# A recurrent loop whose GpSimd subtractions go to VectorE, with another order around them

## The chip, the cores and the metric

One core of a Trainium2 chip runs the kernel. The metric is device time in microseconds. The engines are named as in the profile: PE is the matrix engine (TensorE), DVE is VectorE, ACT is ScalarE, POOL is GpSimd, and SP issues the DMAs.

## The reference, cut to what matters

The model has two layers over 1040 positions (16 meta tokens and 1024 tokens) of width 1024. The first layer is attention and isn't touched here. The second one, in float32, is:

```
def lru_direction(xc, w_a, b_a, w_x, b_x, lam, reverse):
    r = sigmoid(einsum(xc by blocks of 128, w_a) + b_a)
    i = sigmoid(einsum(xc by blocks of 128, w_x) + b_x)
    log_a = -LRU_C * r * softplus(-lam)
    a = exp(log_a)
    b = sqrt(-expm1(2.0 * log_a)) * i * xc
    h[t] = a[t] * h[t-1] + b[t]          # lax.scan over time, reversed for the second direction

def odd_layer(z, w_in, ...):
    u, gate = split_cols(z @ w_in)       # 2048 columns each
    xc = conv_b + centred depthwise convolution of width 4 over u
    y = lru_direction(xc, forward weights) + lru_direction(xc, backward weights, reverse)
    y = y * silu(gate)
    return y @ w_out
```

## The kernel before

The state lies transposed: channels on the 128 partitions, the 1040 positions along a row. Each matmul is done in three passes, so that two fp32r operands give nearly float32: every operand is split into a high part (the value cast to fp32r) and a rest (value minus high part). `wr` is a weight tile as loaded, `wh` and `wl` its high part and rest, `h1h`/`h1l` those of the layer's input, `oxh`/`oxl` those of the convolution's result `oxc`, `oyh`/`oyl` those of a finished row.

The second layer is a loop over e = 0 to 15, one block of 128 channels in each turn (`class Lru`). A turn works on three blocks at once: `cur` is the block e, whose projections are made, `prev` is the block e-1, whose gates are made, and `late` is the block e-2, whose scans are finished. On PE a turn is: `u_mm(0)`, `u_mm(1)`, `prev.gate(0, 0)`, `u_mm(2)`, `prev.gate(1, 0)`, `g_mm(0)`, `prev.gate(0, 1)`, `g_mm(1)`, `prev.gate(1, 1)`. Here u comes in three chunks of about 347 columns (48 matmuls for the first two, 24 for the third), the silu gate in two chunks of 512 (24 each), and each of the four gates takes 9 or 6 matmuls.

The rest of a turn, with its lines in the profile of before:

- `u_out` (L1201, tile `ou`): VectorE evacuates a u chunk times the row's norm. `conv` (L1208 on ScalarE, L1209 to L1211 on VectorE) makes `oxc` after the third.
- `split_xc` (L768 on ScalarE, L769 on VectorE) makes `oxh` and `oxl`.
- `g_in` (L1221, tile `pg`), `silu` (L1224) and `silu_out` (L1228, tile `otg`) make the silu gate of a chunk.
- `gate` (L1254, L1258) is a tanh on ScalarE, `decay` (L1271, L1272) an exp and a tanh, `root` (L1276) the square root, with a load of another function table ahead of it and one behind. `drive` (L1282, tile `tz`), `mul` (L1262) and `scan_in` (L1287, tile `oz`) make the scan's input on VectorE.
- `scan` (L1292 forward, L1294 reverse), `both` (L1299, the sum of the two) and `gated` (L1303, times the silu gate) finish a row. `keep` and `store` send it to DRAM: rows 0 to 7 as high part and rest (L1315 on ScalarE, L1316 on GpSimd), rows 8 to 13 as they are.

The weights of a turn are five loads of 128x512 into three `wr` buffers: two halves of the g weights, the four gate matrices (`wown`), and two halves of the next turn's u weights. `split_w` casts the high part on ScalarE (L113) and takes the rest on GpSimd (L116). Three PSUM banks, taken in turn, hold the u and g chunks.

The order is written out by hand: from e = 1 on, PE, VectorE, ScalarE and GpSimd each run their instructions in the order of the code, and an engine that waits holds up all that stands behind. SP is ordered by a scheduler up to the loop's end, and by the code after it. Behind the loop stand the last two blocks' gates and scans and the output projection (`oo`, 768 matmuls).

Of the kernel before, what the change touches and what calls it, by code (L numbers as in the profile page):

```python
# [7 lines left out]
F32 = mybir.dt.float32  # L8
F32R = mybir.dt.float32r
# [7 lines left out]
P = 128  # L17
# [24 lines left out]
def trunk_kernel(ctx: ExitStack, tc: tile.TileContext, a: dict, out: bass.AP):  # L42
    nc = tc.nc
# [55 lines left out]
    def split_w(src, shape, nm, own=None, eng=nc.gpsimd, own_bufs=1, raw=None):  # L99
        n = 1  # L100
# [10 lines left out]
        with tc.high_priority(sb.get("ahead", 200)):  # L111
# [4 lines left out]
            eng.tensor_sub(lo[:, :n], raw[:, :n], hi[:, :n].bitcast(F32))  # L116
# [1047 lines left out]
    def w_gates(e):  # L1164
        return split_w(a["wg"][e], (4, P), "wg", "gw", own_bufs=2)
# [4 lines left out]
    def w2_half(e, isu, hf):  # L1170
        return split_w(a["w2"][2 * e + isu, hf], (4, P), "w2")

    def w2_load(e, isu):
        return [w2_half(e, isu, hf) for hf in range(2)]
# [11 lines left out]
    class Lru:  # L1186
# [26 lines left out]
        def split_xc(self):  # L1213
            self.c = split(self.xc, "ox", "X")
# [20 lines left out]
        def weights(self):  # L1235
            self.w = w_gates(self.e)
# [73 lines left out]
        def store(self):  # L1310

            e, yv = self.e, self.z[1]
            if e < 8:
                hi, lo = row("oyh", "X", F32R), row("oyl", "X", F32R)
                nc.scalar.copy(hi[:, :1024], yv[:, :1024])  # L1315
                nc.gpsimd.tensor_sub(lo[:, :1024], yv[:, :1024], hi[:, :1024].bitcast(F32))  # L1316
# [45 lines left out]
    for e in range(16):  # L1362
# [5 lines left out]
        if e == 0:  # L1368
# [22 lines left out]
            cur.split_xc()  # L1391
# [5 lines left out]
        else:  # L1397
            w_g = w2_load(e, 0)
            cur.weights()
# [4 lines left out]
            if late:  # L1404
                prev.silu_out(1)
                late.mul(1)
                late.scan_in(1)
            cur.u_mm(1, w_u)
            cur.u_out(1)
            if late:  # L1410
                late.scan(1)
                late.both()
# [7 lines left out]
            if late:  # L1420
                late.gated()
            if e < 15:
                if late:
                    late.keep()
                w_u = [w2_half(e + 1, 1, 0)]
# [3 lines left out]
            if e < 15:  # L1429
                prev.root()  # L1430
                cur.g_in(0, cur.g_mm(0, w_g))
                prev.drive(0)
                prev.drive(1)
                prev.gate(0, 1)
                w_u.append(w2_half(e + 1, 1, 1))
# [4 lines left out]
                cur.split_xc()  # L1440
                if late:
                    late.store()
                cur.g_in(1, cur.g_mm(1, w_g))
                cur.silu(1)
                prev.gate(1, 1)
                late, prev = prev, cur
# [6 lines left out]
    for e in range(4):  # L1453
        y_load(e)
    late.keep()
    cur.split_xc()
# [3 lines left out]
    prev.gate(0, 1)  # L1460
    w_o = [split_w(a["wo2"][d, 0], (4, P), "wo2", raw=raw_o[d]) for d in range(3)]
# [12 lines left out]
    prev.gate(1, 1)  # L1474
# [160 lines left out]
```

## Time and profile before

| | |
|---|---|
| median of 3 runs | 1867.83 us (1867.34 to 1867.99) |
| profiled execution | 1866.78 us, of which the span is 1864.9 us |
| PE busy | 1803.3 us, 97% of the span |
| VectorE busy | 1229.8 us, 66% |
| ScalarE busy | 877.3 us, 47% |
| GpSimd busy | 802.1 us, 43% |
| granted clock of PE | 0.997 |

The span runs from the first instruction to the last; the execution has 1.9 us around it. The recurrent loop with its manual order (e = 1 to 15) takes the stretch from about 1242 to 1675 us, and the output projection follows it. Matmuls overlap, so a busy PE in the table does not say that none of its time is lost. Times in the rows are microseconds from the start of the span.

### The profile page before, as it was taken

How to read it: one execution, taken by the hardware profiler on the slowest of the kernel's cores; microseconds unless marked ns; L12 is line 12 of the kernel's file. 1: busy time of each engine (PE TensorE's matmuls, PEld its weight loads, DVE VectorE, ACT ScalarE, POOL GpSimd, SP SyncE). 2: the span in 40 equal slices, each digit the busy share in tenths (PEclk: the TensorE clock that was granted, in tenths of full speed). 3: DMA queues.
4: the chain of work that ended last, by engine and by line, in shares of the span. 5: the costliest groups of instructions: out<-in, count | busy, mean ns of one | idle time of the engine just before them, and what ended most of it. 6: DMA issues, size and time to landing. Idle time of an engine off the chain costs nothing.

```text
span 1864.9 us, 28561 instructions
## 1 busy us (share of the span) xinstructions
PE 1803.3 (97%) x10822; PEld 1641.8 (88%) x10822; DVE 1229.8 (66%) x1956; ACT 877.3 (47%) x1490; POOL 802.1 (43%) x713
## 2 busy tenths in 40 slices
PE   8999989989999999999999999999999999999999
PEld 7997888889999999888888889998888889988887
DVE  8687357787764641678777774348988989989000
ACT  5455224445443210466667652127776676674000
POOL 5446365354322463357555433332433433326331
PEclk9999999999999999999999999999999999999999
DMA  5355532223222363323222103422222222136421
GB/s 181 81 191 185 164 92 69 62 60 103 61 84 93 137 184 115 117 69 93 70 75 75 41 24 117 145 70 60 76 80 74 95 72 77 60 131 254 143 77 41
DMA packets 109333, 186.47 MB, mean 100 GB/s; under 512 B 31951, under 2 KB 51535, under 8 KB 109198
## 3 DMA queue, kind: packets, MB, share of 16 engines
q1 hardware_dynamic: 109198, 184.67, 31.2%
q8 instruction: 85, 1.39, 0.3%
q14 instruction: 50, 0.41, 0.1%
HBM read 126.72 MB, written 49.92 MB: 95 GB/s over the span
## 4 chain that ended last, share of the span: by engine, by line
PE 69%; DVE 16%; ACT 7%; POOL 5%; issue 2%; DMA 1%; SPq 0%; DVEq 0%; POOLq 0%; ACTq 0%
PE pj L168 12%; PE oo L168 10%; PE pxop L168 6%; PE pg L1183 5%; PE px L935 5%; PE pu L1183 5%; PE av L1026 4%; PE tp L998 3%; PE op L168 3%; PE up L168 3%; PE pz L128 2%; PE vps L435 2%; PE py L935 2%; DVE oxl L769 1%; DVE oz L1287 1%
## 5 line engine op out<-in xcount | busy, mean ns | idle before, releaser
L116 POOL TENSOR_TENSOR wl<-wr,wh 128x512 fp32r<-128x512 f32 (+2 forms) x218 | 320.8, 1475 | 301.9 <-ACT wh L113 269.8
L115 POOL TENSOR_SCALAR wh<-wr 128x512 fp32r<-128x512 f32 (+2 forms) x157 | 121.6, 775 | 376.0 <-PE pj L168 124.4
L168 PE MATMUL pj<-xh,wl 128*128 128x346 f32 (+1 forms) x768 | 251.3, 328 | 14.3 <-DVE wl L116 7.8
L168 PE MATMUL pj<-xl,wh 128*128 128x346 f32 (+1 forms) x768 | 249.1, 324 | 0.9 <-DVE xl L269 0.8
L168 PE MATMUL pj<-xh,wh 128*128 128x346 f32 (+1 forms) x768 | 248.9, 324 | 0.0
L168 PEld LDWEIGHTS pj<-xh,wl 128*128 128x128 f32 x768 | 146.5, 191 | 16.1 <-ACT xh L268 7.7
L168 PEld LDWEIGHTS pj<-xl,wh 128*128 128x128 f32 x768 | 146.6, 191 | 2.0 <-DVE xl L269 1.9
L168 PEld LDWEIGHTS pj<-xh,wh 128*128 128x128 f32 x768 | 146.6, 191 | 0.1
L1183 PE MATMUL pu<-h1h,wl 128*128 128x346 f32 (+1 forms) x384 | 125.2, 326 | 6.3 <-DVE ou L1201 3.3
L1183 PE MATMUL pu<-h1l,wh 128*128 128x346 f32 (+1 forms) x384 | 123.5, 322 | 0.0
L1183 PE MATMUL pu<-h1h,wh 128*128 128x346 f32 (+1 forms) x384 | 123.4, 321 | 0.0
L1013 ACT CAST pth<-tp 128x512 fp32r<-128x512 f32 (+1 forms) x160 | 77.9, 507 | 66.2 <-PE tp L998 52.3
L1014 DVE TENSOR_TENSOR ptl<-tp,pth 128x512 fp32r<-128x512 f32 (+1 forms) x160 | 90.2, 585 | 19.9 <-ACT pth L1013 16.4
L1183 PE MATMUL pg<-h1h,wl 128*128 128x512 f32 x256 | 101.4, 396 | 0.0
L168 PE MATMUL oo<-oyh,wh 128*128 128x512 f32 x256 | 101.1, 395 | 0.0
L1183 PE MATMUL pg<-h1h,wh 128*128 128x512 f32 x256 | 101.1, 395 | 0.0
L1183 PE MATMUL pg<-h1l,wh 128*128 128x512 f32 x256 | 100.8, 394 | 0.0
L168 PE MATMUL oo<-oyh,wl 128*128 128x512 f32 x256 | 100.6, 393 | 0.0
L168 PE MATMUL oo<-oyl,wh 128*128 128x512 f32 x256 | 100.4, 392 | 0.0
L944 ACT ACTIVATE p<-py,mmx,msc 128x256 f32<-128x256 f32 (+1 forms) x72 | 40.8, 567 | 119.0 <-DVE mmx L942 102.3
L1351 DVE TENSOR_TENSOR hres<-oo,hres 128x512 f32<-128x512 f32 x16 | 10.6, 688 | 129.0 <-PE oo L168 129.0
L998 PE MATMUL tp<-ident,p 128*128 128x128 f32 (+1 forms) x576 | 90.5, 275 | 2.7 <-POOL p L955 1.9
(446 smaller groups left out, 5471.2 us busy)
## 6 DMA issues: line engine op xcount, KB each, us to landing
wr<-in_w SPq DMA_DIRECT2D x128, 256.0 KB
wr<-in_wo SPq DMA_DIRECT2D x64, 256.0 KB
s_g<-gth SPq DMA_DIRECT2D x10, 520.0 KB
xr<-in_x SPq DMA_DIRECT2D x8, 520.0 KB
s_qn<-qr SPq DMA_DIRECT2D x8, 520.0 KB
s_kn<-kr SPq DMA_DIRECT2D x8, 520.0 KB
sw<-qraw SPq DMA_DIRECT2D x16, 260.0 KB
yb<-s_yb SPq DMA_DIRECT2D x8, 520.0 KB
```

The source lines that it names most:

```text
L115: eng.tensor_scalar(hi[:, :n], raw[:, :n], 1.0, 1.0, ALU.mult, ALU.mult)
L116: eng.tensor_sub(lo[:, :n], raw[:, :n], hi[:, :n].bitcast(F32))
L128: nc.tensor.matmul(ps[:m, off + c0:off + c1], w, x[:, c0:c1], start=first and j == 0 and pi == 0, stop=last and j == nt - 1 and pi == 2)
L168: nc.tensor.matmul(t[:, :c1 - c0], w, x[:, c0:c1], start=first and j == 0 and pi == 0, stop=last and j == nt - 1 and pi == 2)
L435: nc.tensor.matmul(ps[:m, :n], s, w, start=j == 0 and pi == 0, stop=j == nt - 1 and pi == 2)
L935: nc.tensor.matmul(dst[:m, d0:d0 + a1 - a0], l[:, s], r[:, a0:a1], start=pi == 0, stop=pi == 4)
L944: nc.scalar.activation(p_[:m, b0:b1], ps, AF.Exp, bias=mx[:m, 2:3], scale=sc, accum_out=mx[:m, 3 + z:4 + z])
L998: nc.tensor.transpose(tp[:, o:o + m], p_[:m, NM + P * (kt + j):NM + P * (kt + j) + P], ident[:m, :m])
L1013: nc.scalar.copy(hi[:, :w], tp[:, :w])
L1014: nc.vector.tensor_sub(lo[:, :w], tp[:, :w], hi[:, :w].bitcast(F32))
L1026: nc.tensor.matmul(av[:, :n], l[:, vs], pts[kt][o][:, j * n:j * n + n], start=kt == 0 and j == 0 and pi == 0, stop=False)
L1183: nc.tensor.matmul(t[:, :c1 - c0], l, r[:, c0:c1], start=hf == 0 and k == 0 and pi == 0, stop=hf == 1 and k == 3 and pi == 2)
```

## The change

Four things change in the recurrent loop; the rest of the kernel keeps its instructions and their order.

1. The rests of the five weight tiles of a turn are subtracted on VectorE instead of GpSimd, and so is the rest of a stored row. `split_w` gets a list `later`, into which it puts the subtraction; the loop calls it where it should stand in VectorE's order (`rests[0]` to `rests[4]`). GpSimd keeps one memset of 128x16 a turn.
2. `split_xc` becomes `xc_hi` and `xc_lo`; the last g chunk's `g_in` (the third input chunk of the title) stands between them, and its `silu_out` moves from the next turn to the end of this one.
3. `late.both` moves from behind the reverse scan to behind the third `u_out`, and `late.gated` and `late.keep` to behind the convolution and the fourth rest. The load and cast of the second half of the next u weights move up, from behind `prev.gate(0, 1)` to behind `prev.root`.
4. Behind the loop, `late.gated` stands ahead of the split of the last `oxc`, and `prev.gate(1, 1)` directly behind `prev.gate(0, 1)` instead of behind the last silu.

```
-    def split_w(src, shape, nm, own=None, eng=nc.gpsimd, own_bufs=1, raw=None):
+    def split_w(src, shape, nm, own=None, eng=nc.gpsimd, own_bufs=1, raw=None, later=None):
...
-            eng.tensor_sub(lo[:, :n], raw[:, :n], hi[:, :n].bitcast(F32))
+            rest = lambda e: e.tensor_sub(lo[:, :n], raw[:, :n], hi[:, :n].bitcast(F32))
+            if later is None:
+                rest(eng)
+            else:
+                later.append(lambda: rest(nc.vector))
...
-        def split_xc(self):
-            self.c = split(self.xc, "ox", "X")
+        def xc_hi(self):
+            self.c = row("oxh", "X", F32R), row("oxl", "X", F32R)
+            nc.scalar.copy(self.c[0], self.xc)
+
+        def xc_lo(self):
+            nc.vector.tensor_sub(self.c[1], self.xc, self.c[0].bitcast(F32))
...
-                nc.gpsimd.tensor_sub(lo[:, :1024], yv[:, :1024], hi[:, :1024].bitcast(F32))
+                nc.vector.tensor_sub(lo[:, :1024], yv[:, :1024], hi[:, :1024].bitcast(F32))
...
-            w_g = w2_load(e, 0)
-            cur.weights()
+            rests = []
+            w_g = w2_load(e, 0, rests)
+            cur.weights(rests)
             if late:
                 late.scan(0)
             cur.u_mm(0, w_u)
             cur.u_out(0)
             if late:
-                prev.silu_out(1)
                 late.mul(1)
                 late.scan_in(1)
+            rests[0]()
+            rests[1]()
             cur.u_mm(1, w_u)
             cur.u_out(1)
+            rests[2]()
             if late:
                 late.scan(1)
-                late.both()
...
             cur.u_out(2)
             if late:
-                late.gated()
+                late.both()
             if e < 15:
-                if late:
-                    late.keep()
-                w_u = [w2_half(e + 1, 1, 0)]
+                w_u = [w2_half(e + 1, 1, 0, rests)]
             cur.conv()
             prev.gate(1, 0)
             prev.decay(1)
             if e < 15:
+                rests[3]()
+                if late:
+                    late.gated()
+                    late.keep()
                 prev.root()
+                w_u.append(w2_half(e + 1, 1, 1, rests))
                 cur.g_in(0, cur.g_mm(0, w_g))
                 prev.drive(0)
                 prev.drive(1)
+                rests[4]()
                 prev.gate(0, 1)
-                w_u.append(w2_half(e + 1, 1, 1))
                 cur.silu(0)
                 prev.mul(0)
                 prev.scan_in(0)
                 cur.silu_out(0)
-                cur.split_xc()
+                cur.xc_hi()
+                cur.g_in(1, cur.g_mm(1, w_g))
+                cur.xc_lo()
                 if late:
                     late.store()
-                cur.g_in(1, cur.g_mm(1, w_g))
                 cur.silu(1)
                 prev.gate(1, 1)
+                cur.silu_out(1)
                 late, prev = prev, cur
...
+    late.gated()
     late.keep()
-    cur.split_xc()
+    cur.xc_hi()
+    cur.xc_lo()
...
     prev.gate(0, 1)
+    prev.gate(1, 1)
...
-    prev.gate(1, 1)
     prev.mul(1)
```

What this makes of VectorE's order in the middle of a turn, from the reverse scan (L1294 before, L1302 in the change; both are printed by their operands) to the drives, is seen in two pieces. Before:

```order
L1294 SCALAR_TENSOR_TENSOR oz<-oa,oz 128x1024
L1299 TENSOR_TENSOR oz<-oz 128x1024
L1201 TENSOR_TENSOR ou<-pu,rstd 128x346
L1303 TENSOR_TENSOR oz<-oz,otg 128x1024
L1209 SCALAR_TENSOR_TENSOR oxc<-ou,vec,oxc 128x1038
L1210 SCALAR_TENSOR_TENSOR oxc<-ou,vec,oxc 128x1039
L1211 SCALAR_TENSOR_TENSOR oxc<-ou,vec,oxc 128x1039
L1221 SCALAR_TENSOR_TENSOR pg<-pg,rstd 128x512
L1282 SCALAR_TENSOR_TENSOR tz<-oa,tz 128x1040
L1282 SCALAR_TENSOR_TENSOR tz<-oa,tz 128x1024
```

The same place in the change:

```order
L1302 SCALAR_TENSOR_TENSOR oz<-oa,oz 128x1024
L1205 TENSOR_TENSOR ou<-pu,rstd 128x346
L1307 TENSOR_TENSOR oz<-oz 128x1024
L1213 SCALAR_TENSOR_TENSOR oxc<-ou,vec,oxc 128x1038
L1214 SCALAR_TENSOR_TENSOR oxc<-ou,vec,oxc 128x1039
L1215 SCALAR_TENSOR_TENSOR oxc<-ou,vec,oxc 128x1039
L116 TENSOR_TENSOR wl<-wr,wh 128x512
L1311 TENSOR_TENSOR oz<-oz,otg 128x1024
L1229 SCALAR_TENSOR_TENSOR pg<-pg,rstd 128x512
L1290 SCALAR_TENSOR_TENSOR tz<-oa,tz 128x1040
L1290 SCALAR_TENSOR_TENSOR tz<-oa,tz 128x1024
L116 TENSOR_TENSOR wl<-wr,wh 128x512
```

The third evacuation of u has moved ahead of the sum, the gated product behind the convolution, and two weight rests have come in, one of them behind the drives.

From the end of one turn to the next reverse scan VectorE's order of before is:

```order
L769 TENSOR_TENSOR oxl<-oxc,oxh 128x1040
L1221 SCALAR_TENSOR_TENSOR pg<-pg,rstd 128x512
L1292 SCALAR_TENSOR_TENSOR oz<-oa,oz 128x1040
L1201 TENSOR_TENSOR ou<-pu,rstd 128x348
L1228 SCALAR_TENSOR_TENSOR otg<-otg,pg 128x512
L1262 SCALAR_TENSOR_TENSOR oz<-pz,oxc 128x1024
L1287 TENSOR_TENSOR oz<-oz,tz 128x1024
L1201 TENSOR_TENSOR ou<-pu,rstd 128x346
```

In the change, for a turn that stores a row, the same stretch is:

```order
L1229 SCALAR_TENSOR_TENSOR pg<-pg,rstd 128x512
L1222 TENSOR_TENSOR oxl<-oxc,oxh 128x1040
L1324 TENSOR_TENSOR oyl<-oz,oyh 128x1024
L1236 SCALAR_TENSOR_TENSOR otg<-otg,pg 128x512
L1300 SCALAR_TENSOR_TENSOR oz<-oa,oz 128x1040
L1205 TENSOR_TENSOR ou<-pu,rstd 128x348
L1270 SCALAR_TENSOR_TENSOR oz<-pz,oxc 128x1024
L1295 TENSOR_TENSOR oz<-oz,tz 128x1024
L116 TENSOR_TENSOR wl<-wr,wh 128x512 x2
L1205 TENSOR_TENSOR ou<-pu,rstd 128x346
L116 TENSOR_TENSOR wown<-wr,wown 128x512
```

The last g chunk's evacuation and its silu product have moved ahead of the forward scan, the stored row's rest has come in ahead of it, and three weight rests stand around the second evacuation of u.

On ScalarE, behind the root, the cast of the second half of the next u weights has moved ahead of the table load and the tanh of the next gate. Before:

```order
L1276 ACTIVATE tz<-tz 128x2080
L1258 ACT_TABLE_LOAD
L1258 ACTIVATE pz<-pz,hb 128x1040
L113 CAST wh<-wr 128x512
L1224 ACTIVATE otg<-pg 128x512
```

In the change:

```order
L1284 ACTIVATE tz<-tz 128x2080
L113 CAST wh<-wr 128x512
L1266 ACT_TABLE_LOAD
L1266 ACTIVATE pz<-pz,hb 128x1040
L1232 ACTIVATE otg<-pg 128x512
```

The cast and the tanh have changed places, and the table load stays with the tanh.

## Rows read from the trace of the kernel before

**Rows 1.** Windows: start:end, length, then busy time of each engine.

```profile
1356.80:1386.40 29.60, 28.83 (x151) 25.27 (x151) 26.91 (x22) 20.56 (x22) 11.42 (x7) 1.00 0.24 81
1591.70:1620.10 28.40, 28.40 (x152) 25.35 (x152) 26.25 (x23) 20.52 (x21) 9.33 (x7) 1.00 0.20 65
```

**Rows 2.** Chain of waits: start, length, engine, tile and line.

```profile
1563.59 7.63 PE pu L1183 x48
...
1572.65 3.85 PE pu L1183 x24
...
1648.60 7.63 PE pu L1183 x48
```

**Rows 3.** Timeline of PE, first matmuls of turns e = 1, 4 and 12.

```profile
1242.56 0.32 PE L1183 MATMUL pu<-h1h,wl 128*128 128x348 f32 x1
...
1327.48 0.33 PE L1183 MATMUL pu<-h1h,wl 128*128 128x348 f32 x1
...
1563.43 0.32 PE L1183 MATMUL pu<-h1h,wl 128*128 128x348 f32 x1
```

**Rows 4.** Timeline of PE in turn e = 6: idle time before, and what ended it.

```profile
1388.79 0.43 PE L1183 MATMUL pu<-h1h,wl 128*128 128x348 f32 x1 [0.30 <-POOL wl L116]
...
1396.65 0.43 PE L1183 MATMUL pu<-h1h,wl 128*128 128x346 f32 x1 [0.45 <-DVE ou L1201]
```

**Rows 5.** Timeline of VectorE, turns e = 5 and 6.

```profile
1370.65 2.96 DVE L1294 TENSOR_TENSOR_SCAN oz<-oa,oz 128x1024 f32<-128x1024 f32 x1
1373.64 2.13 DVE L1299 TENSOR_TENSOR oz<-oz 128x1024 f32<-128x1024 f32 x1
1375.70 0.50 DVE L1201 TENSOR_TENSOR ou<-pu,rstd 128x346 f32<-128x346 f32 x1
...
1384.40 2.38 DVE L1282 SCALAR_TENSOR_TENSOR tz<-oa,tz 128x1040 f32<-128x1040 f32 x2 [2.28 <-ACT tz L1276]
1386.82 1.24 DVE L1262 SCALAR_TENSOR_TENSOR oz<-pz,oxc 128x1040 f32<-128x1040 f32 x1
1388.09 1.74 DVE L1287 TENSOR_TENSOR oz<-oz,tz 128x1040 f32<-128x1040 f32 x1
...
1390.36 3.00 DVE L769 TENSOR_TENSOR oxl<-oxc,oxh 128x1040 fp32r<-128x1040 f32 x1
...
1398.36 1.50 DVE L1287 TENSOR_TENSOR oz<-oz,tz 128x1024 f32<-128x1024 f32 x1
...
1405.27 0.50 DVE L1201 TENSOR_TENSOR ou<-pu,rstd 128x346 f32<-128x346 f32 x1
```

**Rows 6.** Timeline of VectorE, turns e = 14 and 15.

```profile
1647.99 1.23 DVE L769 TENSOR_TENSOR oxl<-oxc,oxh 128x1040 fp32r<-128x1040 f32 x1
...
1657.33 2.27 DVE L1294 TENSOR_TENSOR_SCAN oz<-oa,oz 128x1024 f32<-128x1024 f32 x1
1659.63 1.23 DVE L1299 TENSOR_TENSOR oz<-oz 128x1024 f32<-128x1024 f32 x1
```

**Rows 7.** Timeline of GpSimd, turns e = 5 and 6.

```profile
1371.79 2.91 POOL L116 TENSOR_TENSOR wl<-wr,wh 128x512 fp32r<-128x512 f32 x1 [0.28 <-ACT wh L113]
1387.45 1.29 POOL L116 TENSOR_TENSOR wl<-wr,wh 128x512 fp32r<-128x512 f32 x1 [12.75 <-ACT wh L113]
1389.84 2.41 POOL L1316 TENSOR_TENSOR oyl<-oz,oyh 128x1024 fp32r<-128x1024 f32 x1 [1.11 <-ACT oyh L1315]
```

**Rows 8.** Groups of VectorE in the first 60 us: busy time, mean ns.

```profile
L116 DVE TENSOR_TENSOR wl<-wr,wh 128x512 fp32r<-128x512 f32 x2 | 1.4, 688 | 0.0
```

**Rows 9.** Timeline of ScalarE, turn e = 5.

```profile
1371.11 0.60 ACT L113 CAST wh<-wr 128x512 fp32r<-128x512 f32 x1
```

**Rows 10.** Timeline of SP's DMA issues, turn e = 5.

```profile
1367.99 7.06 SPq L96 DMA_DIRECT2D wr<-in_w  x4
```

**Rows 11.** Timeline of VectorE, end of turn e = 15 and behind the loop.

```profile
1668.47 1.24 DVE L769 TENSOR_TENSOR oxl<-oxc,oxh 128x1040 fp32r<-128x1040 f32 x1 [1.13 <-ACT oxh L768]
1671.73 2.38 DVE L1282 SCALAR_TENSOR_TENSOR tz<-oa,tz 128x1040 f32<-128x1040 f32 x2 [2.02 <-ACT tz L1276]
```

More of the change, by code (lines that the diff above doesn't have):

```diff
@@ L1162, in trunk_kernel, with w_gates, w2_half, w2_load @@
     CHR = ((16, 528), (528, 1040))
-    def w_gates(e):
-        return split_w(a["wg"][e], (4, P), "wg", "gw", own_bufs=2)
+    def w_gates(e, later=None):
+        return split_w(a["wg"][e], (4, P), "wg", "gw", own_bufs=2, later=later)
     def halves(t, o=0):
         return [(t[:, 0:512], o, o + 512), (t[:, 512:1024], o + 512, o + 1024)]
[L1170 to L1174, printed above, removed]
+    def w2_half(e, isu, hf, later=None):
+        return split_w(a["w2"][2 * e + isu, hf], (4, P), "w2", later=later)
+    def w2_load(e, isu, later=None):
+        return [w2_half(e, isu, hf, later) for hf in range(2)]
     def chunk_mm(w, halfs, t, c0, c1):
@@ L1233, in g_mm, with weights @@
             return t
-        def weights(self):
-            self.w = w_gates(self.e)
+        def weights(self, later=None):
+            self.w = w_gates(self.e, later)
         def gate(self, d, j):
@@ L1454, in trunk_kernel @@
         y_load(e)
+    late.gated()
     late.keep()
-    cur.split_xc()
+    cur.xc_hi()
+    cur.xc_lo()
     prev.root()
```

## The prediction

> **What bounds the kernel now.** I read the busy times first, then the windows, the chain of waits and the timelines. The matrix engine (PE) is busy in 97% of the span (the table above), so only a stretch where it stands still can give time back. Cut by turn of the recurrent loop, the turn e = 5 takes 29.6 us and PE's modelled busy time is 28.83, while turn e = 13 takes 28.4 with PE busy throughout [rows 1]. The chain of waits shows why: in the late turns it runs through PE alone, and three turns from 1563.59 to 1648.60 take 85.01 us, 28.34 a turn [rows 2]. That is PE's floor, since the change takes no matmul away. The eight turns e = 4 to 11 lie between the PE rows 1327.48 and 1563.43 [rows 3]: 235.95 us against 8 x 28.34 = 226.72. So 9.2 us stand to be won in the whole loop: the three turns before them (1242.56 to 1327.48, 28.31 each) and the last ones are already at the floor.
>
> Where PE stands in such a turn, the PE timeline names [rows 4]. The second half of the next u weights waits for GpSimd's subtraction, and the third u chunk waits for VectorE to evacuate the first chunk (`ou`). That evacuation is late because VectorE's own round is too long. From the third `ou` evacuation (1375.70) to the next one (1405.27) is 29.57 us [rows 5]. Of this, 8.70 us go to ScalarE, which makes the convolution's start, the decays and the root, until `tz` is released at 1384.40; the remaining 20.87 us are one VectorE instruction after another. This round, and not PE, sets the turn.
>
> **GpSimd's part.** The same operations are short where GpSimd is idle [rows 6]: the rest of xc (`oxl`) 1.23 us, the reverse scan 2.27, the sum 1.23. In the long turn they take 3.00, 2.96 and 2.13 [rows 5], each while a GpSimd subtraction of two SBUF tiles runs [rows 7]: `wl` from 1371.79 for 2.91 us lies over scan and sum, `oyl` from 1389.84 for 2.41 over `oxl`. Operations that read PSUM don't show it. The two products (L1287) take 1.74 and 1.50, where I take 1.23, the price of the same shapes undisturbed.
>
> The Trainium skill (SBUF — State Buffer, "Who interferes with whom") says that a VectorE operation with two SBUF inputs and a GpSimd operation that reads SBUF exclude each other, and that whichever starts first keeps the port while the other waits. The trace agrees that they collide, but not on who pays: the scan began at 1370.65, before GpSimd's 1371.79, and still took 2.96. Strictly by that rule the scan's 0.69 excess would not be GpSimd's and would stay: the round worked out below would be 28.57, which leaves 8 x 0.23 = 1.8 us of the loss, a time of 1860.4. The row with GpSimd idle decides, and I take 2.27.
>
> **The new VectorE round, step by step.** Taken off the 20.87: `oxl` 1.77, scan 0.69, the two products 0.51 and 0.27 (1.50 to 1.23). The sum also leaves this stretch: it now stands behind the third `ou`, beside ScalarE's 8.70, so its whole 2.06 goes (1373.64 to 1375.70). Together 5.30.
>
> Added to it: subtractions of 128x512. VectorE's own row for exactly this is 0.688 us [rows 8]; the next instruction begins about 0.07 before the last one ends (1373.64 + 2.13 is 0.07 past 1375.70), so one costs 0.62. The far bound is GpSimd's undisturbed price, 1.29 [rows 7]; I take the near one, since it is the same engine, shape and types. Three stand at the head of the turn: 1.86. The fourth stands behind the convolution beside ScalarE's work. The fifth stands behind the two drives: 2.31 + 0.62 = 2.93 after 1384.40. There the product with xc would wait anyway, because the cast of the second half now lies between root and table load on ScalarE: that wait was 2.42 (1386.82 less 1384.40) and gets about 0.6 longer [rows 5, 9]. So the fifth and that cast together cost 0.6. In turns e = 2 to 9, where a finished row is stored, the rest `oyl` adds 1.23 - 0.08 = 1.15. Sum 3.61.
>
> The round becomes 8.70 + 20.87 - 5.30 + 3.61 = 27.9 us in storing turns, 26.7 in the others. Both lie below 28.34: PE becomes the bound everywhere, with 0.45 us to spare where it is tightest. With the far bound, 1.29 a subtraction, the four would add about 2.5: rounds of 30.4 and 29.2, and a time of about 1879, slower than before. VectorE's own row excludes that as far as a row can.
>
> **What hides the rest.** The first drive stands 8.70 behind the third `ou`. In that time VectorE now has: sum, then from ScalarE's first result (1.8) three convolution steps of 1.3, the fourth subtraction, the gated product (1.2) and the gate's chunk 0.6: 8.2. If that cover went, the excess over 8.70 would be added to the round one for one. Evacuating the third pg chunk ahead of `oxl` moves an instruction of 0.6 within the round and costs nothing. The `silu_out` of that chunk moves ahead of the forward scan. PE's third u chunk, which takes its PSUM bank, starts 9.06 into a turn and lasts 3.85 [rows 2], so the third `ou` stands at 13.1 of a turn; the `silu_out` ends some 18.3 later, at 3.1 of the next turn, 6 us before the bank is wanted. The second stall of rows 4 thus goes. For the first: the last weight rest is now done 8.70 + 2.93 = 11.6 after the third `ou`, at 24.7, and PE wants it in the next turn, after 28.34.
>
> Queues: the loads (`wr`, three buffers) are now released by VectorE. SP issues in order; the tightest one is the next u half, released by the turn's first subtraction at about 8.7 (13.1 + 27.9 less the scan, two subtractions and an evacuation that follow it, 4.0, less 28.34). Its cast on ScalarE stands ahead of the convolution's start and cannot begin before PE has finished the third u chunk, at 13.0. That leaves 4.3 us. Today the load is issued at 1367.99 [rows 10] and cast at 1371.11 [rows 9] without a wait for DMA: at most 3.1. The other four have more.
>
> The end: the last turn's gate moves six matmuls ahead of the second g halves, on the same engine; the gated product (1.2, or 2.3 if GpSimd collides) lies ahead of `oxl`, which idled 1.13 for ScalarE, and the drive behind it idled 2.0 more [rows 11]. I count nothing.
>
> **Sum.** The profiled execution took 1866.78; less 9.2 is 1857.6. The median of the runs is 1.05 higher: 1858.6.
>
> **Rivals.**
> - *VectorE's round stays the longest in storing turns.* For it: only 0.45 us are spare over some 25 instructions. At 0.04 more for each the round is 28.9 and eight turns keep 8 x 0.55 = 4.4 us: 1863.0. Against: nearly every price is a row of this kernel.
> - *A new wait eats the gain.* The change would do its work on VectorE, but PE then waits for a cast or a bank that I counted as early: 1 us a turn in eight turns leaves 1867, the same.
> - *Slower: the load behind the released buffer.* If it lands later than 4.3 + 0.45 us after its issue, each further us delays cast, convolution and round in all turns e = 2 to 14. From 5.5 us on the gain is gone (13 x 0.7 = 9.1), at 6.5 us the time is about 1881. Against: 3.1 is a ceiling, and no wait for a load is seen in these turns.
> - *VectorE stands still after each added instruction.* With its length paid twice (four of 0.69, one of 1.23) the round is 31.9, in the other turns 29.5: 8 x 3.5 + 5 x 1.1 - 9.2 = 24 us slower, 1892. Rows 5 speak against it: the next instruction begins before the last has ended. The Trainium skill (VectorE: DVE Perf Modes, "The DRAIN you can't avoid") says that an idle flush of about the duration less 266 ns follows each operation; no row here shows such a pause.
>
> **How the numbers follow.** Forecast 0.72 (its own range 1857.6 to 1860.4, which takes in the scan's 1.8), longer round 0.14, eaten gain 0.08, late load 0.05, pause 0.01. The range 1857.3 to 1863.2 takes the forecast and most of the longer round. A change of 0.2%, 3.7 us, is about what a measurement can tell here. Faster: 0.72 plus 0.12 of the longer round; same: 0.02 of it plus 0.08; slower 0.06.
>
> **What would show it.** Right: turns of 28.3 us throughout, PE without a stop between the first u chunk and the output projection, `oxl`, sum and scan at 1.23, 1.23 and 2.3, GpSimd with nothing but the 128x16 memsets, VectorE waiting again for PE ahead of the third `ou`. Wrong: `wl` on VectorE above 0.8 us, or ScalarE waiting for a load ahead of a weight cast, or any turn above 28.6.

## The result, and the profile after

| | before | after |
|---|---|---|
| median | 1867.59 us (4 runs) | 1858.22 us (4 runs, 1856.47 to 1859.21) |
| profiled execution | 1866.78 us | 1858.87 us |
| span | 1864.9 us | 1857.1 us |
| granted clock of PE | 0.997 | 0.996 |

The change is faster: the ratio is 0.9949, with a 95% interval of 0.9936 to 0.9963. The medians lie 9.4 us apart, and 1858.6 us had been forecast.

Where the time comes from is read from PE's first matmul of the turns e = 1, 4 and 12, as in [rows 3]. PE's timeline after, with start, length, engine and instruction:

```profile
1242.93 0.32 PE L1187 MATMUL pu<-h1h,wl 128*128 128x348 f32 x1
...
1327.85 0.33 PE L1187 MATMUL pu<-h1h,wl 128*128 128x348 f32 x1
...
1554.26 0.32 PE L1187 MATMUL pu<-h1h,wl 128*128 128x348 f32 x1
```

The eight turns e = 4 to 11 now take 1554.26 - 1327.85 = 226.41 us, 28.30 each, where they took 235.95: 9.54 us. From the turn e = 1 to the turn e = 15 no turn is longer than 28.34 or shorter than 28.27. The windows of the turns e = 5 and 13, the columns as in [rows 1]:

```profile
1356.10:1384.40 28.30, 28.30 (x151) 25.29 (x150) 27.00 (x28) 20.60 (x21) 0.11 (x1) 1.00 0.27 87
1582.70:1611.00 28.30, 28.30 (x151) 25.32 (x151) 25.69 (x28) 19.64 (x20) 0.11 (x1) 1.00 0.21 66
```

PE is busy throughout in both. VectorE's busy time hardly moved in the turn e = 5 (26.91 before, 27.00 after) although six instructions were added to it (x22 to x28), and GpSimd's fell from 11.42 us to 0.11, one memset. VectorE's timeline of the turns e = 5 and 6 answers to [rows 5]; the figure in brackets is the idle time ahead of an instruction and what ended it:

```profile
1366.52 2.28 DVE L1302 TENSOR_TENSOR_SCAN oz<-oa,oz 128x1024 f32<-128x1024 f32 x1
1369.21 0.52 DVE L1205 TENSOR_TENSOR ou<-pu,rstd 128x346 f32<-128x346 f32 x1 [0.41 <-PE pu L1187]
1369.65 1.22 DVE L1307 TENSOR_TENSOR oz<-oz 128x1024 f32<-128x1024 f32 x1
...
1377.93 2.38 DVE L1290 SCALAR_TENSOR_TENSOR tz<-oa,tz 128x1040 f32<-128x1040 f32 x2 [0.56 <-ACT tz L1284]
1380.23 0.68 DVE L116 TENSOR_TENSOR wl<-wr,wh 128x512 fp32r<-128x512 f32 x1
1380.86 1.24 DVE L1270 SCALAR_TENSOR_TENSOR oz<-pz,oxc 128x1040 f32<-128x1040 f32 x1
1382.13 1.24 DVE L1295 TENSOR_TENSOR oz<-oz,tz 128x1040 f32<-128x1040 f32 x1
...
1384.49 1.23 DVE L1222 TENSOR_TENSOR oxl<-oxc,oxh 128x1040 fp32r<-128x1040 f32 x1
1385.64 1.22 DVE L1324 TENSOR_TENSOR oyl<-oz,oyh 128x1024 fp32r<-128x1024 f32 x1
...
1397.52 0.52 DVE L1205 TENSOR_TENSOR ou<-pu,rstd 128x346 f32<-128x346 f32 x1 [0.60 <-PE pu L1187]
```

VectorE now waits for PE ahead of the third `ou` (0.41 and 0.60 us), so the round from one third `ou` to the next, 28.31, is PE's. How long it would be by itself shows in the first two storing turns, where VectorE runs late and waits for nothing there. The same timeline, turns e = 2 to 4:

```profile
1286.00 0.48 DVE L1205 TENSOR_TENSOR ou<-pu,rstd 128x346 f32<-128x346 f32 x1
...
1313.53 0.49 DVE L1205 TENSOR_TENSOR ou<-pu,rstd 128x346 f32<-128x346 f32 x1
...
1341.12 0.49 DVE L1205 TENSOR_TENSOR ou<-pu,rstd 128x346 f32<-128x346 f32 x1
```

The rounds are 27.53 and 27.59 us, 27.56 on the mean, against 29.57 before. The prices, which answer to [rows 6, 8], stand in VectorE's groups by shape, turns e = 2 to 14 (busy time, mean ns of one, idle time before):

```profile
L116 DVE TENSOR_TENSOR wl<-wr,wh 128x512 fp32r<-128x512 f32 x53 | 35.2, 684 | 0.0
L1302 DVE TENSOR_TENSOR_SCAN oz<-oa,oz 128x1024 f32<-128x1024 f32 x13 | 29.7, 2282 | 0.0
L1222 DVE TENSOR_TENSOR oxl<-oxc,oxh 128x1040 fp32r<-128x1040 f32 x14 | 17.2, 1230 | 0.0
L1307 DVE TENSOR_TENSOR oz<-oz 128x1024 f32<-128x1024 f32 x13 | 15.8, 1214 | 0.0
```

The table of waits from 1240 to 1690 us (engine and tile, what it waited for: us in total, times, longest) has no row in which a u or g matmul of PE waits, where [rows 4] stood. ScalarE waited once for a load, in the turn e = 2:

```profile
DVE ou L1205 <- PE pu L1187: 12.1, 11, 1.7
...
ACT wh L113 <- DMA wr<-in_w: 0.7, 1, 0.7
```

Not all of the loop's gain reaches the span, which is 7.8 us shorter. From the first u matmul of e = 1 to that of e = 15 it is 9.68 (405.88 to 396.20). The loop starts 0.37 later in this execution, the stretch from the last turn to the output projection is the same (34.25), and the projection takes 179.25 us instead of 177.87. A new wait stands in it, in PE's timeline:

```profile
1692.19 0.40 PE L172 MATMUL oo<-oyh,wl 128*128 128x512 f32 x1
1693.08 0.50 PE L172 MATMUL oo<-oyl,wh 128*128 128x512 f32 x1 [0.49 <-DMA oyl<-s_yl]
```

These matmuls start every 0.23 us; here the step is 0.89, so 0.66 is lost to the load of a stored row's rest. The other 0.7 of the 1.4 us belongs to no single wait.

### The profile page after: what moved, and what is told of

Read it like the earlier page. It is cut to its first block, busy times and chain, and to the rows that moved or that the text cites. A ratio compares the mean times of both kernels' runs of the same rounds, so it can differ in the third digit from the quotient of the medians.

```text
span 1857.1 us, 28484 instructions
## 1 busy us (share of the span) xinstructions
PE 1801.4 (97%) x10822; PEld 1642.6 (88%) x10822; DVE 1232.5 (66%) x2037; ACT 877.6 (47%) x1490; POOL 660.0 (36%) x632
## 4 chain that ended last, share of the span: by engine, by line
PE 80%; DVE 8%; POOL 5%; ACT 3%; DMA 2%; issue 2%; SPq 0%; DVEq 0%; POOLq 0%; ACTq 0%
PE pj L172 13%; PE pu L1187 10%; PE pg L1187 10%; PE oo L172 9%; PE pxop L172 7%; PE px L939 5%; PE pz L132 5%; PE av L1030 4%; PE tp L1002 3%; PE op L172 3%; PE up L172 3%; PE vps L439 2%; PE py L939 2%; PE av L757 1%; PE sps L697 1%
## 5 line engine op out<-in xcount | busy, mean ns | idle before, releaser
L116 POOL TENSOR_TENSOR wl<-wr,wh 128x512 fp32r<-128x512 f32 (+2 forms) x160 | 229.5, 1436 | 61.6 <-PE pg L1187 49.4
L172 PEld LDWEIGHTS pj<-xh,wl 128*128 128x128 f32 x768 | 147.0, 192 | 14.8 <-ACT xh L272 6.9
```

Source lines behind the costliest of these rows:

```text
L116: rest = lambda e: e.tensor_sub(lo[:, :n], raw[:, :n], hi[:, :n].bitcast(F32))
L172: nc.tensor.matmul(t[:, :c1 - c0], w, x[:, c0:c1], start=first and j == 0 and pi == 0, stop=last and j == nt - 1 and pi == 2)
```

## The experiments

Each kernel was timed beside the kernel before on the same chip, and the ratios to it are what is compared; the median of before shown is that beside the change. "Eight turns" runs from the first u matmul of e = 4 to that of e = 12, "round" from one third `ou` on VectorE to the next in a storing turn in which VectorE doesn't wait for PE there.

| kernel | median, us | ratio (95% interval) | eight turns, us | round, us |
|---|---|---|---|---|
| before | 1867.59 | | 235.95 | 29.57 |
| after | 1858.22 | 0.9949 (0.9936 to 0.9963) | 226.41 | 27.56 |
| `order_only` | 1857.47 | 0.9944 (0.9929 to 0.9959) | 226.41 | 27.52 |
| `vector_only` | 1864.75 | 0.9986 (0.9977 to 0.9995) | 231.23 | 28.97 |
| `sum_only` | 1858.01 | 0.9954 (0.9939 to 0.9968) | 226.41 | 27.39 |
| `sum_line` | 1860.34 | 0.9960 (0.9945 to 0.9974) | 226.41 | 27.40 |
| `sum_back` | 1864.24 | 0.9979 (0.9969 to 0.9989) | 229.79 | 28.88 |
| `waits_only` | 1889.76 | 1.0123 (1.0108 to 1.0138) | 249.24 | 30.97 |
| `one_more` | 1858.06 | 0.9949 (0.9933 to 0.9966) | 226.41 | 28.33 |
| `three_more` | 1875.29 | 1.0046 (1.0029 to 1.0063) | 237.87 | 29.78 |
| `gate_back` | 1860.04 | 0.9957 (0.9942 to 0.9972) | 226.41 | 27.56 |

`row_on_pool` (one execution, 1860.20 us) and `pool_beside_scan` (one, 1858.05 us) have 226.40 and 226.41 us in the eight turns.

### Which half of the change: `order_only` and `vector_only`

`order_only` is the changed kernel with every subtraction back on GpSimd:

```
-                later.append(lambda: rest(nc.vector))
+                rest(eng)
+                later.append(lambda: None)
...
-                nc.vector.tensor_sub(lo[:, :1024], yv[:, :1024], hi[:, :1024].bitcast(F32))
+                nc.gpsimd.tensor_sub(lo[:, :1024], yv[:, :1024], hi[:, :1024].bitcast(F32))
```

> The changed order, but all subtractions (five weight rests, the stored row's rest) left on GpSimd. My theory (a VectorE round that only has to fall below PE's 28.34 us): of the 29.57 the sum's 2.06 goes beside ScalarE, the cast ahead of the table load adds 0.6, so 28.1, up to 28.7 if the sum and the gated product collide with GpSimd: turns of 28.3 to 28.7, time 1858 to 1861. The rival (GpSimd's collisions are what cost the time): oxl at 3.0 and the scan at 2.96 remain, turns of 29 us or more, time 1864 to 1867.

`vector_only` is the kernel before with the subtractions on VectorE, at about the places where they stand in the change (the fifth stands behind the product and the `scan_in` of the forward direction, since its cast comes later in the old order), and everything else in its old place:

```
+                later.append(lambda: rest(nc.vector))
...
-                nc.gpsimd.tensor_sub(lo[:, :1024], yv[:, :1024], hi[:, :1024].bitcast(F32))
+                nc.vector.tensor_sub(lo[:, :1024], yv[:, :1024], hi[:, :1024].bitcast(F32))
...
+            rests[0]()
+            rests[1]()
             cur.u_mm(1, w_u)
             cur.u_out(1)
+            rests[2]()
...
             prev.decay(1)
             if e < 15:
+                rests[3]()
                 prev.root()
...
-                w_u.append(w2_half(e + 1, 1, 1))
+                w_u.append(w2_half(e + 1, 1, 1, rests))
...
                 prev.scan_in(0)
+                rests[4]()
```

> The old order, with the subtractions on VectorE at about the places that the change gives them. My theory: 4.1 us of collisions go (oxl 1.77, sum 0.90, scan 0.69, products 0.78), 3.6 us of subtractions come, round 29.1 instead of 29.57: turns of about 29.1 in e = 4 to 11, time about 1864, so most of the gain is missing. The rival: GpSimd's relief alone is the gain, turns of 28.3, time 1858 to 1859.

The order alone gives the whole gain, with GpSimd as busy as before: all turns are 28.3, and the rival of `order_only` (turns of 29 or more) falls. The engine alone gives half of it in the eight turns (4.7 of 9.5 us) and less of the time: the ratio of 0.9986 is 2.6 us (0.9 to 4.3 by its interval), and the rival of `vector_only` (all of the gain) falls. Its round is 28.97, above PE's 28.3, and PE waits for a weight rest again, as the waits of `vector_only` show:

```profile
PE pu L1187 <- DVE wl L116: 3.3, 8, 0.5
```

So taking GpSimd out is not needed for the gain, and alone it doesn't reach it. What in the order does it had to be found.

### What in the order: `sum_only`, `sum_line`, `waits_only`, `sum_back`

`sum_only` is the kernel before with the sum behind the third `ou`, and the gated product and `keep` (which sends the rows 8 to 13 to DRAM; the expectation calls it the gate's chunk) behind the convolution:

```
                 late.scan(1)
-                late.both()
...
             cur.u_out(2)
             if late:
-                late.gated()
+                late.both()
             if e < 15:
-                if late:
-                    late.keep()
                 w_u = [w2_half(e + 1, 1, 0)]
...
             prev.decay(1)
             if e < 15:
+                if late:
+                    late.gated()
+                    late.keep()
                 prev.root()
...
+    late.gated()
     late.keep()
```

> The kernel before with one thing of the new order alone: the sum (`both`) moves behind the third `ou`, and the gated product and the gate's chunk (`gated`, `keep`) behind the convolution; the subtractions stay on GpSimd, `silu_out(1)` and the u weights' second half stay where they were. Theory (the length of VectorE's round sets the turn): the sum's 2.06 us leave the stretch behind the drives, the round falls from 29.57 to 27.5, below PE's 28.34, and all turns are 28.3: about 1858 us, the whole gain from a few moved lines, and the two waits seen in the turn e = 6 (PE for `wl`, PE for the first `ou`) go although nothing about `wl` or the bank was moved. Rival (those two places, the weight rest and the bank's release, are the cause): they still wait, turns stay at 29 or more, 1864 to 1868 us.

`waits_only` is the kernel before with two other moves instead, those that are meant to take away the two waits of [rows 4] by name:

```
-                prev.silu_out(1)
                 late.mul(1)
...
                 prev.root()
+                w_u.append(w2_half(e + 1, 1, 1))
...
                 prev.gate(0, 1)
-                w_u.append(w2_half(e + 1, 1, 1))
...
                 prev.gate(1, 1)
+                cur.silu_out(1)
```

> The kernel before with the other half of the new order alone: `silu_out(1)` moves from the head of the next turn to the end of its own, and the load, cast and rest of the u weights' second half move ahead of the drives; sum, gated product and chunk stay where they were. VectorE's round keeps all its instructions. Theory (the round sets the turn): the round stays near 29.57, 1.23 above PE's 28.34, so the third `ou` drifts 1.2 us a turn later in its turn as before; PE's stalls can begin a turn or two later because the bank is released earlier, and behind that the turns are 29.6 again: 1861 to 1866 us. Rival (the two named waits are the cause): with them gone all turns are 28.3 and the time is about 1858 us.

`sum_only` has the whole gain. In `waits_only` the round did not stay as I expected: it grew to 30.97, and the turns follow it (about 31 each in e = 4 to 6, then 32.5 and 29.4 in turn). The loop lost 15.9 us on the kernel before and the tail 6.2, so the time missed the expected 1861 to 1866 by far. PE still waits for the weight rest in some turns, and for the very `silu_out` that was issued earlier:

```profile
PE pu L1183 <- DVE otg L1228: 16.0, 12, 1.9
...
PE pu L1183 <- POOL wl L116: 1.0, 5, 0.2
```

VectorE's timeline in it shows where most of the 1.4 us come from, beside GpSimd's:

```profile
1422.43 3.47 DVE L1282 SCALAR_TENSOR_TENSOR tz<-oa,tz 128x1040 f32<-128x1040 f32 x2 [2.28 <-ACT tz L1276]
...
1432.98 0.69 DVE L1228 SCALAR_TENSOR_TENSOR otg<-otg,pg 128x512 f32<-128x512 f32 x1 [0.66 <-ACT otg L1224]
```

```profile
1423.04 1.78 POOL L116 TENSOR_TENSOR wl<-wr,wh 128x512 fp32r<-128x512 f32 x1 [10.31 <-ACT wh L113]
```

The weight rest that was issued earlier now lies on the two drives (3.47 instead of 2.38), and the `silu_out` that was issued earlier waits 0.66 for ScalarE. The two products together change little (1.24 and 1.85, where [rows 5] has 1.74 and 1.50). `waits_only` by itself doesn't test the rival that the two named waits are the cause, since its moves made the round longer. `sum_only` does: it leaves the weight rest and the bank's release where they were, and no u or g matmul of PE waits in it. The two waits were symptoms of the round.

`sum_line` moves one line of the kernel before, and nothing else:

```
                 late.scan(1)
-                late.both()
...
             cur.u_out(2)
             if late:
+                late.both()
                 late.gated()
```

> The kernel before with one line moved: the sum (`both`) from behind the reverse scan to behind the third `ou` evacuation, ahead of the gated product; everything else stays, all subtractions on GpSimd. Theory: in the 8.70 us beside ScalarE VectorE idled 2.3 us (2.98 less 0.69 ahead of the first drive), and the sum's 1.4 fit there, so the round loses the 2.06 that the sum took beside GpSimd and falls to 27.5, below PE's 28.34: all turns 28.3, about 1858 us, all of the change's gain from one line. Rival: the sum delays the convolution's steps by 1.4 us and with them ScalarE's decays or the casts, so the drives start later and the round keeps 1 us or more of it: 28.5 to 28.9, 1858 to 1862.

All turns are 28.3: one line is the change's gain in the loop. Its ratio, 0.9960, lies within the changed kernel's interval; its profiled execution has the loop 1.5 us later in the span than the changed kernel's, and the same 226.41 in the eight turns. The median alone, 1860.34, would also fit the rival, so the trace has to decide. VectorE's timeline from the third `ou` to the drives:

```profile
1399.00 0.52 DVE L1201 TENSOR_TENSOR ou<-pu,rstd 128x346 f32<-128x346 f32 x1 [0.82 <-PE pu L1183]
1399.43 1.21 DVE L1299 TENSOR_TENSOR oz<-oz 128x1024 f32<-128x1024 f32 x1
1400.68 2.20 DVE L1303 TENSOR_TENSOR oz<-oz,otg 128x1024 f32<-128x1024 f32 x1
...
1407.72 2.38 DVE L1282 SCALAR_TENSOR_TENSOR tz<-oa,tz 128x1040 f32<-128x1040 f32 x2 [0.35 <-ACT tz L1276]
```

The drives start 8.72 us behind the third `ou`, where before it was 8.70, so the rival's delay isn't there. [Rows 5] had the reason: ahead of the first drive VectorE stood idle for 2.28 us waiting for ScalarE. Now it waits 0.35, although GpSimd makes the gated product longer (2.20 for 1.21): the sum fills this hole instead of the stretch behind the drives.

`sum_back` is the changed kernel with the sum back behind the reverse scan:

```
                 late.scan(1)
+                late.both()
...
-            if late:
-                late.both()
```

> The changed kernel with the sum back behind the reverse scan, all subtractions on VectorE. The sum then costs its 1.14 in the stretch that nothing covers: round 27.55 + 1.14 = 28.7 us in the eight storing turns, 27.5 in the others, 0.35 above PE's 28.34. Theory (a drift first eats slack): the third `ou` stands at some 15 us behind the turn's first u matmul and moves 0.35 a turn to at most 18; with three more subtractions PE did not yet stop at 16.99 and did at 18.37, so hardly a turn gets longer: 1858 to 1859.5. Rival (what the round exceeds PE's turn by is paid in each turn): 8 x 0.35 = 2.8 us more, 1861.

The third `ou` evacuations and the sum in it, VectorE's timeline:

```profile
1402.53 1.23 DVE L1307 TENSOR_TENSOR oz<-oz 128x1024 f32<-128x1024 f32 x1
1403.67 0.51 DVE L1205 TENSOR_TENSOR ou<-pu,rstd 128x346 f32<-128x346 f32 x1
...
1432.56 0.51 DVE L1205 TENSOR_TENSOR ou<-pu,rstd 128x346 f32<-128x346 f32 x1
```

The round is 28.89 here and 28.88 on the median, 0.2 more than I expected, and the slack is smaller: the third `ou` drifted to 17.7 us behind its turn's first u matmul without a loss, and from 18.3 on six turns took 28.85 to 28.90. The rival's 2.8 us is the nearer figure for the loop. The eight turns lose 3.4 us, and VectorE enters the tail 2.6 us later than in the change, which costs PE 1.6 there. So with all subtractions on VectorE the sum's place is still worth 5 us of the span, in one execution of each.

### How long the round may be: `one_more` and `three_more`

The changed kernel with the third 128x512 subtraction run twice, and four times. The edit of `three_more`:

```
-            rests[2]()
+            for _ in range(4):
+                rests[2]()
```

> The changed kernel with one more 128x512 subtraction a turn on VectorE (the gate weights' rest is taken twice). Theory: the round of 27.9 gets 0.62 longer, 28.5 against PE's 28.3: turns e = 2 to 9 of 28.5, the others unchanged, time 1 to 1.7 us longer, VectorE no longer waiting for PE ahead of the third ou in storing turns. The rival (more slack than I counted): all turns stay at 28.3.

> The changed kernel with the third 128x512 subtraction run four times in each turn, that is three more of 0.69 us. One more made the round 28.33 us, from 27.55 (0.78 for one), and cost nothing. Theory (a round above PE's 28.34 drifts, and stalls PE once the third `ou` stands some 17 to 19 us behind its turn's first u matmul): the round is 27.55 + 3 x 0.62 to 0.78 = 29.4 to 29.9 in the eight storing turns, the others 28.2 to 28.7; the third `ou` starts at some 15 us and drifts 1.1 to 1.6 a turn, so the first two or three storing turns are still 28.3 and the rest are as long as the round: 5 x 1.1 to 6 x 1.6 = 5 to 10 us more than the changed kernel, 1863 to 1868. Rival (VectorE's round has nothing to do with PE's stops; only the order of the waits does): 1858 as before.

One more made the round 28.33, just PE's, and cost nothing; my 28.5 had started from a forecast round that was 0.3 too long. With three more it is 29.78 (three times 0.74; an instruction that repeats the one ahead of it, into the same tile, starts 0.72 behind its start, where the rests otherwise step by 0.60), and PE stops. Its waits:

```profile
PE pu L1187 <- DVE otg L1236: 7.1, 8, 0.9
```

PE waits for the bank of a g chunk, which `silu_out` releases. The eight turns grew by 11.5 us, and the tail by 4.7, since VectorE reaches it that much later. I expected 5 to 10 in all. The added instructions also stand in the turn e = 1, so the third `ou` was at 16.99 at the start of the storing turns, not at 15, and at 18.37 one turn later; the slack was used up at once. That the round sets the turn holds: 29.78, and behind a first one of 29.42 the storing turns take 29.74 to 29.83.

### Who pays in a collision: `pool_beside_scan` and `row_on_pool`

`pool_beside_scan` is the changed kernel with one extra GpSimd operation a turn, beside the reverse scan: in even e the two-input subtraction again, in odd e a one-input multiply of the same size.

```
+                    if one:
+                        nc.gpsimd.tensor_scalar(hi[:, :n], raw[:, :n], 1.0, 1.0, ALU.mult, ALU.mult)
+                    else:
+                        rest(nc.gpsimd)
...
             rests[2]()
+                rests[2](e % 2)
```

> The changed kernel with one more operation on GpSimd in each turn, queued so that it runs beside the first drive to the scans: in even e the subtraction of two SBUF tiles of 128x512 again, in odd e a one-input multiply of 128x512; both write values that are written anyway or equal ones. It is for the price of VectorE's instructions beside each. Theory (GpSimd's two-input operation makes VectorE's SBUF operations longer, whichever started first): in even turns the VectorE instruction that lies under it takes 0.7 to 1.8 us more (the reverse scan 2.96 for 2.28, `oxl` or sum 2.1 to 3.0 for 1.23), in odd turns less or nothing. Rival (the one that starts first keeps its time): only VectorE instructions that start after GpSimd's take longer, and GpSimd's own takes longer where VectorE was first. The time stays near 1858, since the round has 0.8 us to spare and the excess is 0.4 a turn on the mean.

VectorE in the turn e = 2:

```profile
1283.73 2.28 DVE L1308 TENSOR_TENSOR_SCAN oz<-oa,oz 128x1024 f32<-128x1024 f32 x1
1285.93 0.49 DVE L1211 TENSOR_TENSOR ou<-pu,rstd 128x346 f32<-128x346 f32 x1
1286.34 1.85 DVE L1313 TENSOR_TENSOR oz<-oz 128x1024 f32<-128x1024 f32 x1
```

GpSimd beside it:

```profile
1283.95 3.16 POOL L116 TENSOR_TENSOR wown<-wr,wown 128x512 fp32r<-128x512 f32 x1 [49.94 <-DVE wown L116]
```

My theory falls and the rival stands. The scan started 0.22 us ahead of GpSimd and kept its 2.28; GpSimd's subtraction took 3.16 instead of 1.29, and the sum, which started while that ran, took 1.85 instead of 1.21. The trace of before had shown it one GpSimd instruction further back. GpSimd's timeline of before, ahead of [rows 7]:

```profile
1366.67 2.54 POOL L116 TENSOR_TENSOR wl<-wr,wh 128x512 fp32r<-128x512 f32 x2 [3.98 <-PE pz L128]
1369.17 2.29 POOL L116 TENSOR_TENSOR wown<-wr,wown 128x512 fp32r<-128x512 f32 x1
```

The scan of [rows 5] began at 1370.65, while `wown` ran until 1371.46. It waited for that one, not for the `wl` that came at 1371.79; and that `wl` took 2.91 because the scan was first. One sum fits all: a VectorE operation pays GpSimd's remaining time less 0.13. For the scan 1371.46 - 1370.65 - 0.13 = 0.68 (measured 2.96 - 2.27 = 0.69), for the sum 1374.70 - 1373.64 - 0.13 = 0.93 (0.90), for `oxl` 1392.25 - 1390.36 - 0.13 = 1.76 (1.77), for the product 1388.74 - 1388.09 - 0.13 = 0.52 (0.51). In nine of the traces, from 1243 to 1700 us, 419 VectorE operations with two SBUF inputs start while GpSimd works. Of these 411 fit the sum within 0.08 us; the other 8 start at most 0.02 us behind GpSimd and pay nothing. The 442 operations beside GpSimd that read PSUM keep their time within 0.03 us.

`row_on_pool` put this to a forecast: the changed kernel with only `oyl` on GpSimd.

```
-                nc.vector.tensor_sub(lo[:, :1024], yv[:, :1024], hi[:, :1024].bitcast(F32))
+                nc.gpsimd.tensor_sub(lo[:, :1024], yv[:, :1024], hi[:, :1024].bitcast(F32))
```

> The changed kernel with the stored row's rest (`oyl`) back on GpSimd. One rule fits all shared instructions so far: a VectorE operation with two SBUF inputs that starts while GpSimd subtracts takes its own time plus GpSimd's remaining time less 0.13 us, and one that started first keeps its time. By it `oyl` starts on GpSimd at some 14.3 us behind the third `ou` and ends at 16.8, `oxl` starts at 15.28 and takes 1.23 + 16.8 - 15.28 - 0.13 = 2.6 us, and the round is 27.55 - 1.14 + 1.4 = 27.8 in storing turns: below 28.34, so 1858 us. Rival (the two engines slow each other in proportion while they overlap, whoever was first): `oxl` about 2.0 and the scans behind it longer too.

GpSimd, then VectorE, in the turn e = 6:

```profile
1413.67 2.41 POOL L1324 TENSOR_TENSOR oyl<-oz,oyh 128x1024 fp32r<-128x1024 f32 x1 [25.81 <-ACT oyh L1323]
```

```profile
1414.85 2.33 DVE L1222 TENSOR_TENSOR oxl<-oxc,oxh 128x1040 fp32r<-128x1040 f32 x1
1417.10 0.68 DVE L1236 SCALAR_TENSOR_TENSOR otg<-otg,pg 128x512 f32<-128x512 f32 x1
1417.70 2.31 DVE L1300 TENSOR_TENSOR_SCAN oz<-oa,oz 128x1040 f32<-128x1040 f32 x1
```

1416.08 - 1414.85 - 0.13 = 1.10, and 1.23 + 1.10 = 2.33: the measured value. `oyl` started 0.2 us earlier than forecast, so `oxl` paid less than the 2.6 expected. The scan behind it is undisturbed. What `oxl` pays is what VectorE saves on `oyl`, and the turns stay at 28.3. The time of 1860.20 is that of one execution, whose loop starts 2.0 us later in the span than the changed kernel's.

### The tail: `gate_back`

The changed kernel with the last turn's second gate at its old place:

```
-    prev.gate(1, 1)
     w_o = [split_w(a["wo2"][d, 0], (4, P), "wo2", raw=raw_o[d]) for d in range(3)]
...
         cur.silu_out(c)
+    prev.gate(1, 1)
```

> The changed kernel with the last turn's second gate put back to its old place behind the last silu. Theory: the six matmuls moved ahead of the second g halves make PE read the layer's input 1.4 us longer, so the loads that overwrite it land later and PE waits 0.5 to 0.9 us for oyl in the output projection; with the gate back that wait is gone, and the time about 0.7 us lower (too little for the timing, the trace decides). The rival: the wait for oyl comes from the earlier end of the loop as a whole and stays.

I had expected a time lower by 0.7, and the median is not lower (1860.04; the interval of its ratio overlaps with the change's). The wait for `oyl` is gone and the projection takes 178.32 us, but PE waits for ScalarE's tanh instead, in PE's timeline:

```profile
1671.67 0.74 PE L132 MATMUL pz<-oxh,wown 128*128 128x512 f32 x2 [0.96 <-ACT oz L1266]
```

The stretch from the last turn to the projection grows from 34.25 to 35.25. The same wait of 1.0 us stands in `sum_only` and `sum_line`, which leave the gate at its old place, and in none of the five kernels that have it moved and turns of 28.3. So the move of that gate takes a wait of 1 us away. That it brings the wait for `oyl` is not shown: `order_only`, `row_on_pool` and `pool_beside_scan` have the gate moved, too, and PE doesn't wait for `oyl` in their traces (the projection takes 178.49 in each); beside the change only `one_more` shows the wait, with 0.20 lost. With one traced execution of each, its cause stays open. All this is below what the medians can tell.

## Why the prediction was right

**The bound and the prize** were right: the eight turns fell to PE's floor. 226.41 is 0.3 below the 226.72 worked out from the late turns, so 9.54 instead of 9.2.

**VectorE's new round** was forecast at 27.9 and is 27.56. The first part, third `ou` to drives, stayed at 8.7. The rests step by 0.60 each (0.62 forecast), `oyl` adds 1.14 (1.15), the fifth rest with the cast 0.5 (0.6), and scan and sum together gave back 0.1 more than counted: 2.99 + 2.06 became 2.20 (1286.00 less the scan's start at 1283.80), 2.85 for 0.69 + 2.06. No term is off by more than about 0.1, and nearly all err on the long side. Moving the evacuation of the pg chunk cost nothing, as said; the "third" chunk, as it is called ahead of the result, is the second and last g chunk. Four of the rests lie within VectorE's chain and one beside ScalarE, as said.

**The reading of the collision was wrong.** "The trace agrees that they collide, but not on who pays" failed: the scan had found GpSimd at work on an earlier tile. The Trainium skill (SBUF — State Buffer, "Who interferes with whom") says that whichever starts first keeps the port and the other blocks, and the pairs shown here agree (3.16 for GpSimd's 1.29 where the scan was first, 2.33 for VectorE's 1.23 where GpSimd was). The term, 0.69, was still right, since `wown` leaves GpSimd too; the 1860.4 that I worked out "strictly by that rule" applied it to the wrong GpSimd instruction.

**What the gain was put down to** was too wide. The sum of -5.30 and +3.61 is correct, but it hides that its GpSimd part is nearly a wash: with the sum's place changed, the round is 27.52 with the subtractions on GpSimd and 27.56 without. The sum's 2.06 alone would have sufficed, since a round of 27.5 is below 28.34; the one line in the order that fills the idle 2.28 us of [rows 5] is the gain. With the sum left in place the engine's part shortens the round by 0.60 (29.57 to 28.97), which is worth half of the gain in the eight turns and a quarter by the medians.

**The spare of 0.45** was not the edge I took it for. The third `ou` enters the storing turns at 14.8 us behind its turn's first u matmul, and PE's regular stops began with it at 17.2 (a weight rest, `vector_only`, which also has a single stop in its turn e = 2) to 18.3 (a bank, `sum_back`). So a round above 28.34 first uses up some 3 us of slack over the eight turns. The rival of a longer round priced 28.9 at 4.4 us, 8 x 0.55: `sum_back`, at 28.88, lost 3.4 in the loop and 1.6 in the tail, so that price was near, by another sum.

**The other rivals** did not come. No new wait of PE stands in the loop. ScalarE waiting for a load ahead of a weight cast had been named as a sign of being wrong, and it came once, by 0.7, without harm: that cast ended at 1285.54, before the third `ou` at 1286.00. In `vector_only`, `one_more` and `sum_back` it comes in all or nearly all storing turns (up to 2.7 us), and the drives still start 8.6 to 8.7 us behind the third `ou`, as before; so the late load isn't what makes `vector_only` and `sum_back` slower. Where the wait shows, the cast starts 2.6 to 3.0 us behind the load's issue (3.8 once), against the 3.1 that was read as a ceiling. No pause follows an added instruction: a rest is recorded as 0.68 long, and the next instruction starts 0.60 behind its start.

**The tail**, counted at nothing, costs 1.4 us in the profiled execution, of which 0.66 is the new wait for `oyl`. With a loop that starts 0.37 later, it is why 9.7 us won in the loop became 7.8 in the span. The profiled execution was forecast at 1857.6 and took 1858.87. The medians, 9.4 apart, are no better known than by 1 or 2 us: that the forecast of 1858.6 lies 0.4 from 1858.22 is luck in part.

## What to carry to other kernels

Cut the loop by the round of each engine and compare each with the bound's: what has to leave a round is the excess, here 1.2 us, and an idle hole on the same engine can take it at no cost, before any work changes engines. A wait named in the trace can be the symptom of a round that is too long; the moves that were meant to take it away by name made this kernel 1.2% slower. Moving work off GpSimd is little gain in itself: most of what VectorE no longer waits for it then spends on the work itself (4.1 us of collisions for 3.6 us of subtractions, by the count ahead of `vector_only`).

## What the runs showed of the hardware

GpSimd and VectorE don't slow each other in proportion here, where VectorE's operation has two SBUF inputs and GpSimd's reads SBUF: the one that starts second stops until the other's running instruction is nearly over, 0.13 us ahead of its recorded end for VectorE and about 0.2 for GpSimd (1283.95 to the scan's end at 1286.01 is 2.06, and 1.87 was added). GpSimd's one-input multiply beside the scan in the odd turns (2.37 us, where the same operation of this size takes 0.77 on the mean elsewhere in the kernel) waited too, while the scan kept 2.28. The memset, which only writes, took 0.11 and disturbed nothing.
